# A decoder layer on one core: the order of the head's loads, and a fixed order of its work on the engines

## The chip, the cores and the metric

The kernel runs on one core of a Trainium2 chip. A core has five engines with queues of their own: TensorE (PE, with its weight loads as PEld), VectorE (DVE), ScalarE (ACT), GpSimd (POOL) and SyncE (SP), which here issues the DMAs. The metric is the device time of one execution in microseconds, median of several runs. The output has to agree with the float32 reference.

## The reference, cut to what matters

One decoder layer on 512 tokens of 1024 features, batch 1, all in float32:

```
mod = c @ w_ada + b_ada                      # 6 vectors of 1024: shift, scale, gate, twice
h   = rms_norm(x, g_pre_mix) * (1 + sc1) + sh1
proj = h @ w_in                              # [512, 1024] @ [1024, 2268]
o_nsa = nsa_attention(...)                   # 8 heads: compressed, selected and window branch, gated
o_dsa = dsa_attention(...)                   # 8 heads: an indexer picks the top 128 keys for each query
x = x + gt1 * rms_norm(concat(o_nsa, o_dsa) @ w_out, g_post_mix)
h = rms_norm(x, g_pre_ffn) * (1 + sc2) + sh2
y = relu(h @ w_up)**2 @ w_down               # 1024 -> 4096 -> 1024
out = x + gt2 * rms_norm(y, g_post_ffn)
```

The change concerns the way from the inputs to the first two column groups of `proj`: the parts of `mod` for shift and scale, `h`, and `h @ w_in` for the columns 1816 to 2268 ("A") and 512 to 1024 ("B").

## The kernel before, in words

**Arithmetic.** Every float32 matrix product of the projections is made of three passes on rounded operands. Each operand is split into a rounded part and a rest (`split`, L122 to L124: ACT casts the rounded part, DVE subtracts to get the rest), and the passes are rounded by rounded, rounded by rest, and rest by rounded. So each weight block of `w_in` costs a load, a cast on ACT (L123, names uhA, uhB, uh_D, uh_C) and a subtraction on DVE or POOL (L124, ulA, ulB, ul_D). The normalised input `h` is split too: `hh` (ACT, L305) and `hl` (DVE, L307 and L308).

**The head** is everything up to the end of the projections A and B, and it runs in steps k = 0 to 7, one for each slice of 128 of the 1024 features. For one k it does the following.

- `load_mod(k)` loads the columns of `w_ada` for shift and scale of this slice, four pieces of 256 KB (wm, L161). `load_a(k)` and `load_b(k)`, for even k, load the blocks of `w_in` for two slices (rwA 452 KB, L166; rwB 512 KB, L170).
- `mod_sums(k)` multiplies `c` with them on PE (mp, L286, 8 float32 matmuls that the profile shows as 16) and ACT copies the result out (macc, L291). `mod_mm(k)` sums over partitions with two small matmuls (mp, L297, shown as 4).
- `mod_h(k)`: DVE adds the bias and multiplies by the norm's weight (`as`, L301 and L302); with that as scale and bias ACT makes `hh` from the transposed slice xT, and DVE makes `hl`.
- `proj_pass` (L323): pA, 12 matmuls of 452 columns (3 passes by 4 row tiles), for step k; and pB, 9 matmuls of 512 columns (3 passes by 3 row tiles), for the step before. pB's fourth row tile comes behind the head, as pj_B.

Ahead of the loop x is loaded in four row tiles, squared and summed on ACT (L258), scaled on DVE (L262) and transposed on PE in 32 blocks (xTp, L268), with copies to xT on ACT (L269). Six of the eight slices are transposed as the row tiles come; slices 6 and 7 get a PSUM bank later.

**Behind the head** come pj_B, then the projections of the column chunks D (1024 to 1304), C (0 to 512) and E (1304 to 1816), each from `w_in_chunk` (loads L770), then the attention branches, the output projection and the MLP.

**What sets the order.** The program is written in Python calls, and a scheduler with a simulated timeline decides the order of the instructions on each engine from their dependences; in `before` it moves nearly all of them, the loads on SP too. `tc.issue_after(x)` makes what is emitted under it stand behind x; `tc.keep_in_program_order` keeps an instruction in the order of the program. Work of later stages is put into numbered slots of the program by the table PLAN and `place`. Buffers come from pools: `unit` (10 buffers of 512 KB), `raw` (4), k4 for x, and PSUM banks S (4), T (2) and O (2). A load waits until its buffer is free, and SP's queue stands at it meanwhile. Each DMA also waits for the DMA eight places ahead of it.

Of the kernel before, what the change touches and what calls it, by code (L numbers as in the profile page):

```python
# [69 lines left out]
def layer_kernel(  # L70
# [74 lines left out]
    for t in range(NT):  # L145
        xt = k4(f"x_{t}", F32)
        xs.append([xt[:, 0], xt[:, 1]])
        for i in range(2):
            SY.dma_start(xs[t][i], xv[t][:, i * 512:i * 512 + 512])
            if small:  # L150
                SY.dma_start(*small.pop(0))
# [113 lines left out]
    def x_transpose(k, tag):  # L265
        ps = bank(tag, f"xTp_{k}")
        for t in range(NT):
            last = PE.transpose(ps[:, t * P:(t + 1) * P], xs[t][k // 4][:, (k % 4) * P:(k % 4 + 1) * P], ident)  # L268
        A.copy(xT[k], ps)  # L269
        return last.ins  # L270
# [8 lines left out]
    def mod_sums(k):  # L279
# [11 lines left out]
        A.copy(acc, pv)  # L291
        macc[k] = (ps, acc)

    def mod_mm(k):
        ps, acc = macc[k]
        for v in range(2):
            PE.matmul(ps[:, 256 + v:257 + v], acc[:, v, :], ones32, start=True, stop=True)  # L297
        return ps[:, 256:258]

    def mod_h(k, ps):  # L300
# [4 lines left out]
        A.activation(hh[:, :, k, :], xT[k].rearrange("p (t q) -> p t q", q=P), AF.Identity,  # L305
                     scale=as1[:, 1, k:k + 1], bias=as1[:, 0, k:k + 1])
        V.tensor_scalar(h32, xT[k], as1[:, 1, k:k + 1], as1[:, 0, k:k + 1], op0=OP.mult, op1=OP.add)  # L307
        return lambda: V.tensor_tensor(hl[:, :, k, :], h3, hh[:, :, k, :].bitcast(F32), op=OP.subtract)  # L308
# [11 lines left out]
    def proj_pass(ps, t, k, w, n, i):  # L320
        hi, lo = w[k // 2]
        l, r = ((hh, hi), (hh, lo), (hl, hi))[i]
        PE.matmul(ps[:, :n], l[:, t, k, :], r[:, k % 2, :n],  # L323
                  start=(k == 0 and i == 0), stop=(k == KT - 1 and i == 2))
# [8 lines left out]
    mod_sums(0)  # L333
    last = [x_transpose(k, "S") for k in range(4)][-1]
    with tc.issue_after(last):
        mp = mod_mm(0)
    split_a(0)
    rt_ops = rope_tables()
    psA = [bank("S", f"pA_{t}") for t in range(NT)]
    psB = []  # L340
    for k in range(KT):
        mod_h(k, mp)()
        if k + 1 < KT:
            mod_sums(k + 1)
        if k + 3 < KT:
            if k % 2 == 1:
                load_a(k + 1)
            load_mod(k + 3)
            if k % 2 == 1:
                load_b(k + 1)  # L350
        if k % 2 == 1 and k + 1 < KT:
            if k + 3 >= KT:
                load_a(k + 1)
                load_b(k + 1)
            split_a(k + 1)
        if k % 2 == 0:
            split_b(k)
# [224 lines left out]

    def cmp_load(nm):
# [180 lines left out]
    def w_in_chunk(c0, c1, nm, eng=V):  # L764
# [16 lines left out]
    for f in lD:  # L781
        f()
# [12 lines left out]
    for t in range(NT + 2):  # L795
# [8 lines left out]
        sD=sD, cl=[lambda: cmp_load("k"), lambda: cmp_load("v")], lC=lC, sC=sC, lE=lE, sE=sE,  # L804
# [5 lines left out]
        tk1=tk[1], tk2=tk[2], tk3=tk[3], g1=g1s, a2=a2s, sh2=sh2s)  # L810
# [389 lines left out]
```

## Time and profile before

| | us |
|---|---|
| median of 3 runs | 730.72 (730.03 to 732.52) |
| the profiled execution | 730.62, of which the span from the first to the last instruction is 728.9 |
| head: first pA matmul, first of pj_B | 23.53, 76.99 |
| busy: PE, DVE, ACT, POOL | 686.2, 458.0, 331.8, 128.9 |

A row of the timeline reads: start, length, engine, line, operation, output<-inputs, shapes, count, and in brackets how long the engine was idle before it and for what. "PE mp L286 <- DVE as L301: 2.5, 3, 1.5" in the waits means that PE stood 2.5 us in 3 waits ahead of such matmuls, 1.5 at the longest, until an `as` of DVE was there. In the windows view, the clock is the rate granted to PE as a share of its full one; waits and chain name the program's tiles with their numbers left out.

### The profile page before, as it was taken

The numbers are of one execution on the slowest core, as the hardware profiler recorded it, in microseconds if no ns is written. First come the engines' busy times: TensorE is split into PE (matmuls) and PEld (weight loads), VectorE is DVE, ScalarE is ACT, GpSimd is POOL, SyncE is SP. The second block draws the span as 40 slices with busy tenths as digits, with TensorE's granted clock in tenths as the row PEclk, the third lists the DMA queues.
The fourth block names the chain that finished last, engine by engine and source line by source line (L and its number), as shares of the span: only waits on it lengthen the run. The fifth ranks groups of instructions, "written<-read, shape, count | busy, mean of one in ns | idle before, by whom it ended". The sixth has DMA issues, their size and how long they took to land.

```text
span 728.9 us, 9985 instructions
## 1 busy us (share of the span) xinstructions
PE 686.2 (94%) x3601; PEld 535.1 (73%) x3601; DVE 458.0 (63%) x978; ACT 331.8 (46%) x691; POOL 128.9 (18%) x196
## 2 busy tenths in 40 slices
PE   4898989979998999799999999999999999999995
PEld 2676978857664666465699888888888888788884
DVE  4345548989998989775675463653734455443547
ACT  5343685534896569644564323232331332323222
POOL 3000195635524125122020000000000000000003
PEclk9999999999998999999999999999999999999998
DMA  8997430422316761462123351533424133331202
GB/s 246 300 304 246 115 88 2 114 69 78 117 27 176 176 144 29 121 227 87 58 88 103 101 169 63 174 115 116 147 60 169 58 116 115 89 114 59 86 1 115
DMA packets 67611, 87.15 MB, mean 120 GB/s; under 512 B 3973, under 2 KB 38889, under 8 KB 67562
## 3 DMA queue, kind: packets, MB, share of 16 engines
q1 hardware_dynamic: 67562, 86.52, 39.6%
q8 instruction: 28, 0.46, 0.3%
q14 instruction: 21, 0.17, 0.1%
HBM read 84.40 MB, written 2.10 MB: 119 GB/s over the span
## 4 chain that ended last, share of the span: by engine, by line
PE 74%; DVE 12%; DMA 4%; POOL 3%; issue 2%; ACT 2%; SPq 2%; POOLq 0%; DVEq 0%; ACTq 0%
PE up L1113 23%; PE dn L1154 22%; PE op L1006 6%; PE O L905 3%; PE pj_E L323 3%; PE pA L323 2%; DMA wm<-in_w_ada_dram 2%; PE pj_C L323 2%; DVE wk L570 1%; PE pB L323 1%; DVE m L567 1%; SPq L161 1%; PE tp_d L899 1%; DVE P_d L894 1%; DMA rwA<-in_w_in_dram 1%
## 5 line engine op out<-in xcount | busy, mean ns | idle before, releaser
L1113 PE MATMUL up<-hh,uh_U 128*128 128x512 f32 (+1 forms) x288 | 104.6, 366 | 0.6 <-ACT hh L123 0.6
L1113 PE MATMUL up<-hh,ul_U 128*128 128x512 f32 (+1 forms) x288 | 104.9, 366 | 0.0
L1113 PE MATMUL up<-hl,uh_U 128*128 128x512 f32 (+1 forms) x288 | 104.0, 366 | 0.0
L1154 PE MATMUL dn<-uh_D,al 128*128 128x512 f32 x256 | 99.6, 389 | 0.0
L1154 PE MATMUL dn<-uh_D,ah 128*128 128x512 f32 x256 | 98.7, 391 | 0.0
L1154 PE MATMUL dn<-ul_D,ah 128*128 128x512 f32 x256 | 98.5, 389 | 0.0
L124 DVE TENSOR_TENSOR ul_D<-rw_D,uh_D 128x1024 fp32r<-128x1024 f32 (+1 forms) x35 | 41.2, 1180 | 47.5 <-ACT uh_D L123 45.4
L1160 DVE TENSOR_TENSOR y<-dn,y 128x512 f32<-128x512 f32 x56 | 38.1, 688 | 48.6 <-PE dn L1154 48.6
L206 POOL TENSOR_SCALAR ms<-sy 128x1 f32<-128x1 f32 x4 | 3.6, 909 | 341.6 <-ACT fj L1133 341.6
L1113 PEld LDWEIGHTS up<-hh,uh_U 128*128 128x128 f32 x288 | 54.3, 188 | 9.7 <-ACT hh L123 0.9
L1117 ACT ACTIVATE rl<-up 128x512 f32<-128x512 f32 x32 | 19.1, 596 | 92.7 <-PE dn L1154 59.2
L1113 PEld LDWEIGHTS up<-hh,ul_U 128*128 128x128 f32 x288 | 54.3, 189 | 8.8
L1113 PEld LDWEIGHTS up<-hl,uh_U 128*128 128x128 f32 x288 | 53.7, 189 | 8.9 <-DVE hl L124 0.2
L123 ACT CAST uh_U<-rw_U 128x1024 fp32r<-128x1024 f32 x32 | 33.6, 1051 | 55.2 <-PE dn L1154 51.9
L123 ACT CAST uh_D<-rw_D 128x1024 fp32r<-128x1024 f32 (+1 forms) x36 | 36.3, 1010 | 46.2 <-PE up L1113 37.5
L1154 PEld LDWEIGHTS dn<-uh_D,al 128*128 128x128 f32 x256 | 48.1, 188 | 10.2 <-issue 0.2
L1154 PEld LDWEIGHTS dn<-uh_D,ah 128*128 128x128 f32 x256 | 48.1, 188 | 10.2 <-issue 0.2
L1154 PEld LDWEIGHTS dn<-ul_D,ah 128*128 128x128 f32 x256 | 48.0, 188 | 10.0
L124 DVE TENSOR_TENSOR ul_U<-rw_U,uh_U 128x1024 fp32r<-128x1024 f32 x32 | 39.1, 1221 | 10.9 <-ACT uh_U L123 10.0
L1118 DVE TENSOR_TENSOR rl<-rl 128x512 f32<-128x512 f32 x32 | 22.0, 689 | 34.9 <-ACT rl L1117 34.9
L123 ACT CAST ah<-rl 128x512 fp32r<-128x512 f32 x32 | 19.9, 621 | 29.3 <-DVE rl L1118 29.2
L124 DVE TENSOR_TENSOR al<-rl,ah 128x512 fp32r<-128x512 f32 x32 | 22.0, 688 | 11.0 <-ACT ah L123 11.0
(407 smaller groups left out, 1473.4 us busy)
## 6 DMA issues: line engine op xcount, KB each, us to landing
rw_U<-in_w_up_dram SPq DMA_DIRECT2D x32, 512.0 KB, 4.5
rw_D<-in_w_down_dram SPq DMA_DIRECT2D x32, 512.0 KB, 3.7
wm<-in_w_ada_dram SPq DMA_DIRECT2D x32, 256.0 KB, 6.3
wv_g<-in_w_ada_dram SPq DMA_DIRECT2D x8, 512.0 KB, 4.6
rwo_a<-in_w_out_dram SPq DMA_DIRECT2D x16, 256.0 KB, 4.9
wv_a<-in_w_ada_dram SPq DMA_DIRECT2D x8, 512.0 KB, 3.7
rwo_b<-in_w_out_dram SPq DMA_DIRECT2D x16, 256.0 KB, 4.9
wv_sh<-in_w_ada_dram SPq DMA_DIRECT2D x8, 512.0 KB, 4.2
```

The source lines that it names most:

```text
L123: A.copy(hi, src)
L124: eng.tensor_tensor(lo, src, hi.bitcast(F32), op=OP.subtract)
L161: mod_in[k].append(SY.dma_start(wt[hf][:, v], wa[:, hf * 4:hf * 4 + 4, v * D + k * P:v * D + (k + 1) * P]))
L323: PE.matmul(ps[:, :n], l[:, t, k, :], r[:, k % 2, :n], start=(k == 0 and i == 0), stop=(k == KT - 1 and i == 2))
L567: mx = V.max(m8, work[t])
L905: mm = [PE.matmul(O[j][g * 64:(g + 1) * 64, :], vn[kb][:, self.vsl[g]:self.vsl[g] + 64], pts[kb, g][0], start=(first and kb == 0), stop=(l ...
L1006: PE.matmul(stt["ps"], l[:, kk, :], r[:, kk % 2, :], start=(kk == 0 and i == 0), stop=(kk == 7 and i == 2))
L1113: PE.matmul(pv[:, t0:t1, :], l[:, k % 2, fs], r[:, t0:t1, k, :], start=(n == 0), stop=(n == 23))
L1117: A.activation(rl, ps, AF.Relu)
L1118: V.tensor_tensor(rl, rl, rl, op=OP.mult)
L1154: PE.matmul(ps, l[:, t * P:(t + 1) * P], r[:, f % 2, :], start=(n == 0), stop=(n == 11))
L1160: V.tensor_tensor(ya, ps, ya, op=OP.add)
```

## The change

Four things are changed, all in or around the head.

1. The loads. x comes in four loads of a whole row tile (512 KB) instead of eight halves, and the six small loads go from SP's queue to ACT's. The loads of wm, rwA and rwB stay in the order of the program, which is now wm0, rwA0, wm1, rwB0, wm2, rwA2, wm3, rwB2 and so on to rwB6. The loads of chunk D stand behind rwB6; those of the compression weights (`cl`) and of the output gate (`g1`: g and wv_g) behind D's last, C's behind these.
2. The transposes. The copies of xT alternate between ACT (even k) and DVE (odd k). In the program the transposes of slices 1 to 3 stand behind `mod_h(0)`.
3. The order in the loop. `behind(done, f)` emits f under `issue_after` of each instruction of `done`. `mod_mm(k+1)` is put behind the last pA matmul of step k, the nine pB behind that, and the sums of the step after next ahead of the following row of pA; for k = 0 and 1 the sums stand behind the second pass. The splits of the next A and B blocks stand behind `mod_h`, and those of chunk D behind the last `mod_h`.
4. `x_transpose`, `mod_sums`, `mod_mm`, `mod_h`, `load_b`, `proj_pass` and the chunk's `load` return the instructions that this needs. The arithmetic is the same.

```diff
-        for i in range(2):
-            SY.dma_start(xs[t][i], xv[t][:, i * 512:i * 512 + 512])
-            if small:
-                SY.dma_start(*small.pop(0))
+        SY.dma_start(xt.rearrange("p a n -> p (a n)"), xv[t])
+    for dst, src in small:
+        A.dma_start(dst, src)
...
-                mod_in[k].append(SY.dma_start(wt[hf][:, v], wa[:, hf * 4:hf * 4 + 4, v * D + k * P:v * D + (k + 1) * P]))
+                src = wa[:, hf * 4:hf * 4 + 4, v * D + k * P:v * D + (k + 1) * P]
+                mod_in[k].append(tc.keep_in_program_order(SY.dma_start(wt[hf][:, v], src)))
...
-        A.copy(xT[k], ps)
-        return last.ins
+        return A.copy(xT[k], ps) if k % 2 == 0 else V.tensor_copy(xT[k], ps)
...
+    def behind(done, f, *args):
+
+        with ExitStack() as es:
+            for ins in done:
+                es.enter_context(tc.issue_after(ins.ins))
+            return f(*args)
+
+    first = mod_sums(0)
+    first_T = x_transpose(0, "S")
+    mp, _ = mod_mm(0)
+    behind((first, first_T), split_a, 0)
...
     for k in range(KT):
-        mod_h(k, mp)()
-        if k + 1 < KT:
-            mod_sums(k + 1)
+        done = mod_h(k, mp)
+        if k == 0:
+            for q in (1, 2, 3):
+                behind(done, x_transpose, q, "S")
+            psA = [bank("S", f"pA_{t}") for t in range(NT)]
+        if k % 2 == 0 and k + 2 < KT:
+            load_a(k + 2)
+        elif k % 2 == 1 and k + 1 < KT:
+            head_end = (load_b(k + 1),)
         if k + 3 < KT:
             load_mod(k + 3)
...
+        if 1 < k < KT - 1:
+            mod_sums(k + 1)
         for ps in (0, 1, 2):
             for t in range(NT):
-                proj_pass(psA[t], t, k, wA, 452, ps)
+                mm = proj_pass(psA[t], t, k, wA, 452, ps)
+            if k < 2 and ps == 1:
+                done += (behind((mm,), mod_sums, k + 1),)
+        if k % 2 == 0:
+            behind(done, split_b, k)
+        elif k + 1 < KT:
+            behind(done, split_a, k + 1)
...
         if k + 1 < KT:
-            mp = mod_mm(k + 1)
+            mp, mm = behind((mm,), mod_mm, k + 1)
         for t in range(3):
             if k > 0:
-                proj_mm(psB[t], t, k - 1, wB, 512)
+                behind((mm,), proj_mm, psB[t], t, k - 1, wB, 512)
...
+    d_loads = [behind(head_end, f) for f in lD]
+    sD = [lambda f=f: behind(done, f) for f in sD]
...
-        sD=sD, cl=[lambda: cmp_load("k"), lambda: cmp_load("v")], lC=lC, sC=sC, lE=lE, sE=sE,
+        sD=sD, cl=[held(lambda: cmp_load("k")), held(lambda: cmp_load("v"))], lC=lC, sC=sC, lE=lE, sE=sE,
```

Here `held(f)` is `behind` with the last load of D. How the rows stand on the engines now is shown at three places; numbers behind a name are buffer numbers.

On PE, at the start, where the transposes (xTp) of the last two x tiles meet the first sums (mp from wm). Before:

```order
L268 MATMUL xTp_276<-ident,x_82 128x128
L268 MATMUL xTp_282<-ident,x_82 128x128
L268 MATMUL xTp_202<-ident,x_87 128x128
...
L268 MATMUL xTp_282<-ident,x_87 128x128
L286 MATMUL mp_191<-wm_90,c_sb 32x256 x4
L286 MATMUL mp_191<-wm_91,c_sb 32x256 x4
L297 MATMUL mp_191<-ones_113,macc_200 128x1 x2
```

and with the change (x_76 and x_78 are the last two tiles):

```order
L268 MATMUL xTp_280<-ident,x_74 128x128
L285 MATMUL mp_187<-wm_86,c_sb 32x256 x4
L285 MATMUL mp_187<-wm_87,c_sb 32x256 x4
L268 MATMUL xTp_198<-ident,x_76 128x128
...
L268 MATMUL xTp_274<-ident,x_78 128x128
L268 MATMUL xTp_280<-ident,x_78 128x128
L296 MATMUL mp_187<-ones_109,macc_196 128x1 x2
```

The first sums stood behind the transposes of all four tiles and now stand ahead of those of the last two.

On PE in the loop, at the end of step 3 and the start of step 4, where the sums' last matmul (L297, now L296) meets pA, pB and the next sums. Before:

```order
L323 MATMUL pA_236<-uhA_323,hl_177 128x452
L323 MATMUL pB_349<-uhB_386,hl_177 128x512
L323 MATMUL pB_350<-uhB_386,hl_177 128x512
L323 MATMUL pB_351<-uhB_386,hl_177 128x512
L297 MATMUL mp_423<-ones_113,macc_432 128x1 x2
L286 MATMUL mp_500<-wm_380,c_sb 32x256 x4
L286 MATMUL mp_500<-wm_381,c_sb 32x256 x4
L323 MATMUL pA_233<-uhA_444,hh_176 128x452
```

and with the change:

```order
L323 MATMUL pA_238<-uhA_335,hl_173 128x452
L296 MATMUL mp_452<-ones_109,macc_461 128x1 x2
L323 MATMUL pB_345<-uhB_400,hh_172 128x512
...
L323 MATMUL pB_347<-uhB_400,hl_173 128x512
L285 MATMUL mp_510<-wm_367,c_sb 32x256 x4
L285 MATMUL mp_510<-wm_368,c_sb 32x256 x4
L323 MATMUL pA_235<-uhA_475,hh_172 128x452
```

Between the sums' last matmul and the next pA stood the next sums alone; now the nine pB and the sums stand there.

On SP, the loads of the second half of the head. Before:

```order
L161 DMA wm_380<-in_w_ada_dram 128x4x128 x2
...
L736 DMA g_1617<-in_g_post_mix_dram 128x1024
L711 DMA wv_g_1623<-in_w_ada_dram 128x4x256
L161 DMA wm_436<-in_w_ada_dram 128x4x128 x2
L711 DMA wv_g_1628<-in_w_ada_dram 128x4x256
L161 DMA wm_381<-in_w_ada_dram 128x4x128 x2
L166 DMA rwA_434<-in_w_in_dram 128x2x452
...
L770 DMA rw_D_696<-in_w_in_dram 128x2x280
L161 DMA wm_512<-in_w_ada_dram 128x4x128 x2
L166 DMA rwA_567<-in_w_in_dram 128x2x452
L170 DMA rwB_569<-in_w_in_dram 128x2x512
```

and with the change:

```order
L166 DMA rwA_496<-in_w_in_dram 128x2x452
L161 DMA wm_498<-in_w_ada_dram 128x4x128 x2
L161 DMA wm_499<-in_w_ada_dram 128x4x128 x2
L170 DMA rwB_554<-in_w_in_dram 128x2x512
L782 DMA rw_D_692<-in_w_in_dram 128x2x280
...
L748 DMA g_1613<-in_g_post_mix_dram 128x1024
L723 DMA wv_g_1619<-in_w_ada_dram 128x4x256
L723 DMA wv_g_1624<-in_w_ada_dram 128x4x256
L782 DMA rw_C_764<-in_w_in_dram 128x2x512
```

The loads g and wv_g and the first of D stood among the head's loads; now the last of the head's, rwB6, stands ahead of D, and D ahead of g, wv_g and C.

More of the change, by code (lines that the diff above doesn't have):

```diff
@@ L165, in load_a @@
         raw_a[k] = unit(f"rwA{k}", F32)
-        SY.dma_start(raw_a[k][:, :, :452], wiv[:, k:k + 2, 1816:2268])
+        tc.keep_in_program_order(SY.dma_start(raw_a[k][:, :, :452], wiv[:, k:k + 2, 1816:2268]))
     def load_b(k):
         raw_b[k] = unit(f"rwB{k}", F32)
-        SY.dma_start(raw_b[k], wiv[:, k:k + 2, 512:1024])
+        return tc.keep_in_program_order(SY.dma_start(raw_b[k], wiv[:, k:k + 2, 512:1024]))
     load_mod(0)
@@ L267, in x_transpose @@
         for t in range(NT):
-            last = PE.transpose(ps[:, t * P:(t + 1) * P], xs[t][k // 4][:, (k % 4) * P:(k % 4 + 1) * P], ident)
-        A.copy(xT[k], ps)
-        return last.ins
+            PE.transpose(ps[:, t * P:(t + 1) * P], xs[t][k // 4][:, (k % 4) * P:(k % 4 + 1) * P], ident)
+        return A.copy(xT[k], ps) if k % 2 == 0 else V.tensor_copy(xT[k], ps)
     hh = ht("hh", "hh_1")
@@ L290, in mod_sums @@
         acc = m2(f"macc_{k}")[:, 0:256].rearrange("p (v n) -> p v n", v=2)
-        A.copy(acc, pv)
         macc[k] = (ps, acc)
+        return A.copy(acc, pv)
     def mod_mm(k):
@@ L296, in mod_mm @@
         for v in range(2):
-            PE.matmul(ps[:, 256 + v:257 + v], acc[:, v, :], ones32, start=True, stop=True)
-        return ps[:, 256:258]
+            mm = PE.matmul(ps[:, 256 + v:257 + v], acc[:, v, :], ones32, start=True, stop=True)
+        return ps[:, 256:258], mm
     def mod_h(k, ps):
@@ L322, in proj_pass @@
         l, r = ((hh, hi), (hh, lo), (hl, hi))[i]
-        PE.matmul(ps[:, :n], l[:, t, k, :], r[:, k % 2, :n],
-                  start=(k == 0 and i == 0), stop=(k == KT - 1 and i == 2))
+        return PE.matmul(ps[:, :n], l[:, t, k, :], r[:, k % 2, :n],
+                         start=(k == 0 and i == 0), stop=(k == KT - 1 and i == 2))
     def proj_mm(ps, t, k, w, n):
@@ L332, in layer_kernel @@
     columns()
[L333 to L337, printed above, removed]
+    def behind(done, f, *args):
[7 more added lines that the diff above has]
+    behind((first, first_T), split_a, 0)
     rt_ops = rope_tables()
-    psA = [bank("S", f"pA_{t}") for t in range(NT)]
     psB = []
     for k in range(KT):
-        mod_h(k, mp)()
-        if k + 1 < KT:
-            mod_sums(k + 1)
+        done = mod_h(k, mp)
[7 more added lines that the diff above has]
+            head_end = (load_b(k + 1),)
         if k + 3 < KT:
-            if k % 2 == 1:
-                load_a(k + 1)
             load_mod(k + 3)
[L349 to L357, printed above, removed]
         for _ in range(4):
@@ L581, in layer_kernel, with held @@
     csrc = {"k": (cmp_pe_k, cmp_w1_k, cmp_w2_k), "v": (cmp_pe_v, cmp_w1_v, cmp_w2_v)}
+    def held(f):
+        return lambda: behind(d_loads[-1:], f)
     def cmp_load(nm):
@@ L809, in layer_kernel @@
         ck3=[lambda: cmp_gelu("k"), lambda: cmp_out("k")], cv3=[lambda: cmp_gelu("v"), lambda: cmp_out("v")],
-        tk1=tk[1], tk2=tk[2], tk3=tk[3], g1=g1s, a2=a2s, sh2=sh2s)
+        tk1=tk[1], tk2=tk[2], tk3=tk[3], g1=[held(f) for f in g1s[:3]] + g1s[3:], a2=a2s, sh2=sh2s)
     slots = {n: [] for n in range(40)}
```

9 lines of the change are left out of this document (4 added, 5 removed).

## The prediction, made before the changed kernel ran

> **What bounds the kernel now.** I read the page's totals first, then the windows view, the waits of the stretch in question, its chain of waits and its timeline.
>
> ```profile
> span 728.9 us, 9985 instructions
> PE 686.2 (94%) x3601; PEld 535.1 (73%) x3601; DVE 458.0 (63%) x978; ACT 331.8 (46%) x691; POOL 128.9 (18%) x196
> ```
>
> TensorE is busy 94% of the span. A gain of some size must come from PE's idle time or from time at a lower clock. The windows view says where those lie. The columns are the window, its length, the busy time (with the instruction count) of PE, weight loads, DVE, ACT and POOL, the granted clock, the DMA share and the GB/s.
>
> ```profile
> 29.55:64.00 34.45, 31.72 (x211) 24.41 (x209) 16.36 (x31) 15.05 (x23) 1.76 (x1) 1.00 0.99 291
> 64.00:68.00 4.00, 4.00 (x19) 3.25 (x12) 1.34 (x2) 1.01 (x3) 0.00 (x0) 0.59 0.97 342
> 68.00:77.00 9.00, 7.63 (x38) 6.55 (x37) 2.01 (x5) 3.00 (x6) 0.00 (x0) 0.99 0.20 76
> 140.00:320.00 180.00, 165.70 (x981) 110.79 (x980) 160.13 (x491) 116.25 (x308) 66.99 (x82) 0.95 0.42 116
> ```
>
> ```profile
> 29.14 0.66 PE L268 MATMUL xTp<-ident,x 128*128 128x128 f32 x4
> 29.55 1.06 PE L323 MATMUL pA<-uhA,hh 128*128 128x452 f32 x4
> 76.99 0.39 PE L323 MATMUL pj_B<-uhB,hh 128*128 128x512 f32 x1
> ```
>
> These rows of the timeline (start, length) give the borders: step k=1 of pA begins at 29.55, and the head is over at 76.99, 47.44 us later, when pj_B begins. From 29.55 on PE is idle for 2.73 us before 64 and for 1.37 us after 68, in sum 4.10. In 64 to 68 it runs at 0.59, which costs 0.41 of 4.00 = 1.64 us. So 5.74 us of the head after 29.55 are neither work nor full clock. The two waits named for PE there add up to the idle time:
>
> ```profile
> PE mp L286 <- DVE as L301: 2.5, 3, 1.5
> PE pA L323 <- ACT hh L305: 1.6, 2, 1.4
> ```
>
> The chain of waits shows how they come about (start, length, what):
>
> ```profile
> 42.13 6.25 DMA rwA<-in_w_in_dram
> 48.46 0.94 ACT uhA L123
> 49.41 0.73 ACT hh L305
> 50.18 1.92 PE pA L323 x8
> ...
> 52.44 0.94 PE pA L323 x4
> 53.37 2.21 PE pB L323 x9
> 55.58 1.00 PE mp L286 x16
> ...
> 58.43 1.39 PE pB L323 x6
> ...
> 61.35 0.35 PE mp L297 x4
> 61.70 1.38 DVE ul_D L124 x2
> 63.08 0.08 DVE as L301
> ...
> 71.46 0.82 ACT hh L305
> ...
> 77.16 0.92 PE pj_B L323 x4
> ```
>
> Three stalls. At 48 us ACT stands at the cast of rwA4, whose load landed late, and hh of that step queues behind it. At 61.70 the vector `as` queues on DVE behind two splits of chunk D that nobody needs yet, and the next sums wait for it. At 71.46 the last hh stands in the chain itself: between the last mm and the pA of step 7 no pB is left to cover it.
>
> **The change, part by part.** *The loop from pA(1) on.* The directly ordered loop puts mod_mm(k+1) behind the twelve pA of step k, then nine pB and the next sums. After the mm the next step needs `as` and hh, about 0.36 + 0.81 and the hand-overs, 1.5 us in all. Nine pB (2.21) and one sums (1.00) are 3.2 us of cover; before, the mm often stood last and had one sums, 1.0, as cover. So the waits on `as` and hh should go, which removes 4.10 us, and with the idle of 1.52 us ahead of it the slow window (1.64) probably goes too: it is the only slow one in the head. If it does not, the gain is 1.64 smaller; that end is in the range. DVE keeps its splits, but behind `hl`, and D's behind the last `hl`: they move to where the next `as` is 3 us away.
>
> Does the data come in time? A step takes 2.7 (pA: 1.92 + 0.94, the shorter repeats less) + 2.2 + 1.0 + 0.35 = 6.2 us. It needs four pieces of wm, 1.05 MB, and half of one rwA and one rwB (loads with their KB and the us to landing; then the GB/s in slices of 2.25 us from 0 to 90):
>
> ```profile
> wm<-in_w_ada_dram SPq DMA_DIRECT2D x32, 256.0 KB, 6.3
> rwA<-in_w_in_dram SPq DMA_DIRECT2D x4, 452.0 KB, 7.2
> wv_g<-in_w_ada_dram SPq DMA_DIRECT2D x2, 512.0 KB, 5.6
> GB/s 29 242 277 217 252 314 330 303 325 313 290 291 291 327 339 261 235 215 313 332 329 321 332 321 346 367 294 137 201 349 373 20 0 0 0 256 320 291 65 0
> ```
>
> With rwB's 512 KB that is 1.05 + 0.24 + 0.26 = 1.55 MB in 6.2 us, 250 GB/s; the row of 29.55 to 64 moved 291. Before, the two wv_g (1.05 MB, 3.6 us at 291), g and D's first chunk ran ahead of rwA6 and rwB6; now they stand behind. So I price the supply at nothing, with the transfers behind the work as cover; the bound, if it moved only the 217 GB/s of a slow slice at the start, is 1.55/0.217 = 7.1 us a step, 0.9 us times six steps = 5.4 us lost.
>
> From pA(1) to the head's end the after program also has work that before stood ahead of pA(1): six pB of k=0 (1.39), sums(2) (1.00) and the transposes of slice 7 (0.6). So this part takes 47.44 - 4.10 - 1.64 + 1.39 + 1.00 + 0.60 = 44.7 us.
>
> *The start, up to pA(1).* Here the rows are (start, length):
>
> ```profile
> 1.24 0.42 SPq L151 DMA_DIRECT2D c_sb<-in_c_dram  x1
> 14.82 1.54 PE L268 MATMUL xTp<-ident,x 128*128 128x128 f32 x6 [2.02 <-DVE x L262]
> 16.29 1.94 PE L286 MATMUL mp<-wm,c_sb 128*32 128x256 f32 x16
> 18.77 1.01 PE L297 MATMUL mp<-ones,macc 128*128 128x1 f32 x4 [0.55 <-ACT macc L291]
> 19.89 0.16 DVE L301 TENSOR_TENSOR as<-mp,colb 128x2 f32<-128x2 f32 x1 [2.44 <-PE mp L297]
> 20.17 1.10 DVE L124 TENSOR_TENSOR ulA<-rwA,uhA 128x904 fp32r<-128x904 f32 x1
> 20.34 0.81 ACT L305 ACTIVATE hh<-xT,as 128x512 fp32r<-128x512 f32 x1 [0.78 <-DVE as L302]
> 21.18 0.54 DVE L307 TENSOR_SCALAR h<-xT,as 128x512 f32<-128x512 f32 x1
> 21.83 0.69 DVE L308 TENSOR_TENSOR hl<-h,hh 128x512 fp32r<-128x512 f32 x1
> 28.14 1.07 PE L286 MATMUL mp<-wm,c_sb 128*32 128x256 f32 x16
> ```
>
> The new order has sums(0) ahead of the transposes of x tiles 2 and 3 (12 rows, 2 x 1.54). Sums(0) starts when wm0 has landed: x and wm0 are 3.15 MB, at some 0.28 MB/us (the slices from the second on) from about 2 us that is 13.4; the bound on the other side is 16.3, where it stood. From it: 1.94 + 3.08 + 1.01 and `as` give hh0 at 19.9 to 22.8, against 20.34. To pA(1): hl0 is 2.25 us behind the start of hh0 (0.54 + 1.10 + 0.69), then pass 3 of two tiles and the five pA behind it (1.6), sums(1) 1.07, one pA 0.22, a transpose group 0.6, the mm 0.35, and the open chain to hh1 of 1.5, since at k=0 no pB stands there yet: 7.55 us. So pA(1) comes at 27.45 with PE at full rate and wm0 early. [...] I take the middle, 28.6, with 27.45 and 32.7 (late and slow) as bounds.
>
> [...]
>
> *The loads at the top.* x in four loads instead of eight and the small ones on ACT's queue: ten issues fewer on SP, 0.42 us each, 4.2 in all. What it is worth is within wm0's 13.4 to 16.3: the 9.5 us for x's bytes cover the issues of wm0 in the early case. On ACT the six issues, 2.5 us, stand ahead of the squares of x; that can make tile 0 up to 2.5 us later, but tile 3 waits for its bytes, so 0. *xT copies*: four of 0.6 us go from ACT to DVE, three of them ahead of as(1); they run under pA(0) and sums(1), so 0, and at most 0.6 if the last is still running when mm(1) ends.
>
> *What is behind the head.* PE's order is the same from pj_B on for 217 rows, through pj_D and pj_C, and again through the whole MLP; only in between are rows shuffled. So an earlier head end should carry through.
>
> ```profile
> 74.28 1.05 ACT L123 CAST uh_C<-rw_C 128x1024 fp32r<-128x1024 f32 x1 [2.01 <-PE pA L323]
> 89.03 0.32 POOL L401 TENSOR_TENSOR ra_Bc<-pjB,rsin 128x64 f32<-128x64 f32 x1 [28.33 <-PE skp_kA L417]
> ```
>
> POOL's rope waits for PE's skp_kA at 89 and so follows the head. The danger is C: its loads now stand behind g, wv_g and w_k and need D's buffers, and the cast of C0 on ACT has copies of pA banks behind it, which pj_D needs. I estimate C0 between the new head end and 2.4 us behind it; the banks are needed 5 us behind it, so 0, with 1 us as bound.
>
> **The sum.** pA(1) 28.6 + 44.7 = 73.3, against 76.99: 3.7 us earlier. The profiled execution took 730.62 (span 728.9 and 1.7 around it); the median of the runs, 730.72, is the same. Forecast 730.6 - 3.7 = **726.9**.
>
> **The rivals.** *PE at full rate at once*: 27.45 + 44.7 = 72.15, 4.8 gained, 725.8. [...] Against: the row of 16.29 with transposes just ahead of it. *The start eats the gain*: wm0 lands only at 16.3 and sums(0) has 12 transposes behind it instead of in front. pA(1) then stands at 30.3 (warm) to 32.7 (slow), the head ends 75.0 to 77.4: 728.6 to 731.0, in the middle 729.8. For it: before had all tiles done at 16.36 and sums running at once. Against: the slices above show no stop of the DMA before 16, and wm0 had ten issues more ahead of it.
>
> *The loads do not keep up* (the order is there, its data not): the 217 GB/s case, 5.4 - 3.7 = 1.7 lost, about 732.3; against it, most slices of the loop stand at 290 or above, though one shows 215. *Slower through the middle*: from 140 to 320 DVE is busy 160.1 of 180 and PE idle 14.3; the rows of DVE, ACT and PE are shuffled a little there. If DVE's new order opens two more gaps like that at 61.70, each with 1.52 idle and a 0.59 window of 1.64, 6.3 us go: 730.6 - 3.7 + 6.3 = 733.2. It decides from 3.7 us on. For it: that stretch's clock of 0.95 says such windows come easily (0.05 x 180 = 9 us). Against: the moves are of a few rows each, and could close a gap as well.
>
> **Chances.** Forecast 0.47 (726.9), warm at once 0.15 (725.8), start 0.18 (729.8), loads 0.06 (732.3), middle 0.14 (733.2). 0.3%, 2.2 us, is about what a measurement of this kernel tells from no change: 728.5 and 732.9 are the borders. Faster 0.61 (the first two, less a little), same 0.25, slower 0.14. The range: 722.8 (warm, and 3 us closed in the middle) to 732.0 (late and slow start, 1 us for C); the forecast's own is 725.8 (27.45) to 728.2 (29.9).
>
> **What would show it.** Right: pj_B's first matmul at 72 to 75; no wait of mp on `as` and at most one, 1.5 us at k=0, of pA on hh; the granted clock at 1.00 from 29 to the head's end; rwB6's landing by some 52 us; the rows from 77 on the same distance earlier through 320. The start is right if hh0 stands at 19.9 to 20.5 and pA(1) near 28.6. Wrong: pA(1) past 31, a wait on a wm load, ACT standing at uh_C for over 5 us, or a PE idle time from 140 to 320 well above 14.3, with the head's gain then gone again by 320.

## The result, and the profile after

The changed kernel takes 726.04 us (median of 14 runs, 724.12 to 730.4) against 730.56 us of the kernel before on the same chip (14 runs, 728.59 to 732.79). The ratio is 0.9942, with a 95% interval of 0.9921 to 0.9962. The forecast was 726.9 in a range of 722.8 to 732.0, faster. The profiled execution took 724.70. Three slow executions, two of the kernel before (739.96 and 1127.28 us) and one of the kernel with the sums of step 1 early (1121.82), are in no median or mean below.

The totals of its page:

```profile
span 723.0 us, 9982 instructions
PE 684.1 (95%) x3601; PEld 532.8 (74%) x3601; DVE 460.8 (64%) x982; ACT 328.6 (45%) x687; POOL 131.8 (18%) x196
```

The windows view (window, length, busy time of PE, weight loads, DVE, ACT, POOL, granted clock, DMA share, GB/s) shows the loop as it was meant: PE busy for all of 44 us, at full clock.

```profile
20.00:29.00 9.00, 7.54 (x63) 5.28 (x64) 4.24 (x8) 3.72 (x6) 0.00 (x0) 1.00 1.13 317
29.00:73.00 44.00, 44.00 (x267) 34.77 (x266) 23.86 (x49) 17.96 (x32) 1.40 (x1) 1.00 0.87 252
```

In the waits view from 23 to 75 us, PE has one wait left, that of the open chain to step 1, and ACT stands for 5.8 us ahead of the cast of C:

```profile
ACT uh_C L123 <- DMA rw_C<-in_w_in_dram: 5.8, 1, 5.8
...
PE pA L323 <- ACT hh L304: 1.5, 1, 1.5
```

The chain of waits in the same stretch is PE alone, in the order that the change wrote down (sums' last matmul L296 behind pA, nine pB, the next sums L285):

```profile
56.37 1.00 PE mp L285 x16
57.37 2.67 PE pA L323 x12
60.04 0.34 PE mp L296 x4
60.37 2.17 PE pB L323 x9
62.55 2.47 PE pA L323 x12
65.02 4.13 PE pB L323 x18
69.15 5.45 PE pj_B L323 x24
```

The first pj_B matmul stands at 68.98, 8.0 us earlier than before. The span is only 5.9 us shorter. The first instances of the same tiles on PE say where the rest went: pj_D is 8.0 us earlier (74.42 against 82.46), the first of pj_E 8.3 (126.81 against 135.14), the first tp_d of the attention's last part, those that read hh_d, 5.7 (276.07 against 281.73), and from there on the lead stays at 5.7 to 5.9. So the lead is carried whole to the middle, and 2.85 us of it are lost between sc, the first scores of the compressed branch (172.17 before, 163.66 after), and tp_d. The windows of this stretch, before:

```profile
172.17:193.75 21.58, 20.63 (x134) 15.78 (x133) 19.76 (x76) 14.30 (x47) 12.86 (x22) 0.92 0.19 63
193.75:241.78 48.03, 44.44 (x269) 27.22 (x266) 45.43 (x156) 37.50 (x107) 15.78 (x17) 0.93 0.48 121
241.78:281.73 39.95, 39.33 (x228) 27.02 (x228) 33.40 (x92) 27.71 (x69) 11.25 (x12) 1.00 0.47 120
```

and after, between the same tiles:

```profile
163.66:187.61 23.95, 22.23 (x137) 17.08 (x136) 21.47 (x80) 14.76 (x48) 13.20 (x22) 0.86 0.14 45
187.61:236.75 49.14, 45.03 (x265) 27.79 (x265) 43.86 (x154) 36.69 (x102) 15.80 (x17) 0.90 0.42 125
236.75:276.07 39.32, 39.08 (x228) 26.82 (x227) 34.14 (x92) 28.04 (x71) 12.35 (x12) 1.00 0.46 113
```

I call length x (1 - granted clock) the clock loss. It is 1.73 + 3.36 = 5.1 us in this stretch before and 3.35 + 4.91 = 8.3 us after. The difference, 3.2 us, is more than the 2.85 us; PE's idle time is 5.2 and 6.1.

At the start the sums of step 0 and what follows them stand like this (timeline: start, length):

```profile
12.75 1.92 PE L285 MATMUL mp<-wm,c_sb 128*32 128x256 f32 x16
14.60 1.53 PE L268 MATMUL xTp<-ident,x 128*128 128x128 f32 x12
15.96 0.50 PE L296 MATMUL mp<-ones,macc 128*128 128x1 f32 x4
17.03 0.81 ACT L304 ACTIVATE hh<-xT,as 128x512 fp32r<-128x512 f32 x1
24.82 1.09 PE L323 MATMUL pA<-uhA,hh 128*128 128x452 f32 x4 [1.46 <-ACT hh L304]
```

The sums still ran at about half rate (1.92 us, where the next ones, at 21.11, take 1.07), the twelve transposes behind them at full rate: 1.53 us, where the forecast had 3.08.

### The profile page after: what moved, and what is told of

The parts are those of the page before. It is cut to its first block, busy times and chain, and to the rows that moved or that the text cites. A ratio compares the mean times of both kernels' runs of the same rounds, so it can differ in the third digit from the quotient of the medians.

```text
span 723.0 us, 9982 instructions
## 1 busy us (share of the span) xinstructions
PE 684.1 (95%) x3601; PEld 532.8 (74%) x3601; DVE 460.8 (64%) x982; ACT 328.6 (45%) x687; POOL 131.8 (18%) x196
## 4 chain that ended last, share of the span: by engine, by line
PE 76%; DVE 11%; DMA 4%; ACT 4%; POOL 3%; issue 2%; POOLq 0%; ACTq 0%; SPq 0%; DVEq 0%
PE up L1125 23%; PE dn L1166 22%; PE op L1018 5%; PE pA L323 3%; PE pj_E L323 3%; PE O L917 3%; PE pB L323 2%; DVE wk L578 1%; DVE m L575 1%; DMA rwo_b<-in_w_out_dram 1%; PE mp L285 1%; PE tp_d L911 1%; PE pj_C L323 1%; PE tp_s L911 1%; DMA wv_g<-in_w_ada_dram 1%
## 5 line engine op out<-in xcount | busy, mean ns | idle before, releaser
L1129 ACT ACTIVATE rl<-up 128x512 f32<-128x512 f32 x32 | 19.1, 598 | 92.6 <-PE dn L1166 59.2
L1166 PEld LDWEIGHTS dn<-uh_D,al 128*128 128x128 f32 x256 | 48.1, 188 | 10.2 <-issue 0.2
```

The costliest lines, as they stand in the source:

```text
L1129: A.activation(rl, ps, AF.Relu)
L1166: PE.matmul(ps, l[:, t * P:(t + 1) * P], r[:, f % 2, :], start=(n == 0), stop=(n == 11))
```

## The experiments

All are edits of the changed kernel. The table has the ratio to the kernel before on the same chip; where pA of step 1 and pj_B begin in the one profile; and, as means over all timed runs, the clock loss and the time without it (time - span x (1 - granted clock)). That last figure must be read with care: up to the moment at which a trace first records full rate (14.5 us in the first profile of the change, 23.8 before, 5.7 in the kernel with PE warmed) the clock's record says 1.00 although the durations show about half rate (sums of 1.92 and 1.94 us that take 1.07 later in the first two, transposes of 0.42 us that take 0.27 later in the third), so that part of a slow start counts as time without clock loss.

| kernel | median us | ratio [95%] | pA(1) | pj_B | clock loss | time without it |
|---|---|---|---|---|---|---|
| before (three sets of runs on two chips, 17 to 29 each) | 731.2 to 733.0 | 1 | 29.55 | 76.99 | 16.2 to 17.6 | 714.9 to 715.8 |
| the change, first runs | 726.04 | 0.9942 [0.9921, 0.9962] | 24.82 | 68.98 | 18.1 | 708.5 |
| the change again | 726.91 | 0.9938 [0.9919, 0.9957] | 27.93 | 73.61 | 18.4 | 708.6 |
| x in halves | 730.41 | 0.9968 [0.9942, 0.9994] | 28.72 | 72.88 | 17.0 | 713.3 |
| small loads on SP | 729.23 | 0.9959 [0.9938, 0.9979] | 27.41 | 71.58 | 17.8 | 711.4 |
| first sums last | 725.44 | 0.9929 [0.9904, 0.9954] | 26.46 | 70.64 | 16.4 | 710.1 |
| xT copies on ACT | 726.89 | 0.9931 [0.9907, 0.9956] | 27.33 | 73.02 | 19.0 | 708.7 |
| sums' last matmul behind pB | 729.54 | 0.9961 [0.9931, 0.9990] | 25.89 | 74.74 | 18.7 | 711.5 |
| engine order free | 728.54 | 0.9947 [0.9920, 0.9974] | - | 76.42 | 16.8 | 711.9 |
| loads' order free | 730.16 | 0.9964 [0.9933, 0.9996] | 27.65 | 73.33 | 19.7 | 710.6 |
| no holding back | 729.41 | 0.9965 [0.9948, 0.9982] | 26.93 | 72.64 | 19.1 | 710.2 |
| PE warmed | 727.56 | 0.9943 [0.9928, 0.9958] | 26.16 | 71.83 | 20.2 | 707.2 |
| sums of step 1 early | 724.99 | 0.9896 [0.9873, 0.9919] | 24.12 | 68.29 | 14.6 | 709.6 |
| the same again | 723.12 | 0.9881 [0.9861, 0.9900] | 25.01 | 69.18 | 14.6 | 708.8 |

### The changed kernel once more

No edit.

> The changed kernel once more, unaltered, on the chip of the runs beside it. If its gain lies in the head and in work and idle time, not in luck with the clock (theory A), the time without what the lower clock costs (span x (1 - granted clock)) is about 708.5 again, some 6 us below the same figure of the kernel before, pA of step 1 begins between 24.8 and 27.7, and the loop takes 44.2 us and 1.7 more for each slow-clock stretch in it. If the 69.0 of the first profile was luck (rival), pj_B stands past 72.

The loop takes 73.61 - 27.93 = 45.68 us, 1.5 more than in the first profile, and PE is never idle in it; the start is 3.1 us later. Timeline and windows of this execution show why (the same program, the same order):

```profile
13.10 1.93 PE L285 MATMUL mp<-wm,c_sb 128*32 128x256 f32 x16 [0.76 <-DMA wm<-in_w_ada_dram]
14.96 2.82 PE L268 MATMUL xTp<-ident,x 128*128 128x128 f32 x12
...
18.79 0.81 ACT L304 ACTIVATE hh<-xT,as 128x512 fp32r<-128x512 f32 x1 [0.60 <-DVE as L301]
```

```profile
20.00:24.00 4.00, 4.00 (x15) 2.48 (x18) 2.74 (x5) 0.56 (x2) 0.00 (x0) 0.66 1.11 314
24.00:28.00 4.00, 2.54 (x26) 1.56 (x18) 1.39 (x4) 2.52 (x4) 0.00 (x0) 0.91 1.12 318
28.00:32.00 4.00, 4.00 (x24) 2.71 (x24) 1.23 (x3) 0.00 (x0) 0.00 (x0) 0.57 1.15 305
```

The twelve transposes take 2.82 instead of 1.53, and PE runs at about half rate in two more stretches up to 32. Both readings have a part: the time without clock loss is 708.6 as expected, and pj_B past 72 says that the 69.0 of the first profile was a lucky start. These two profiles of the head differ by 4.6 us, so a single one can't be trusted to less than that.

### x in halves again

```diff
-        SY.dma_start(xt.rearrange("p a n -> p (a n)"), xv[t])
-    for dst, src in small:
-        A.dma_start(dst, src)
+        for i in range(2):
+            SY.dma_start(xs[t][i], xv[t][:, i * 512:i * 512 + 512])
+            if small:
+                SY.dma_start(*small.pop(0))
```

> The changed kernel, but x comes in eight halves with the six small loads between them on SP again; by that the sums of step 0 fall behind the transposes of all four x tiles again. With the change, pA of step 1 begins at 24.82 us and pj_B at 68.98. If the start gained by the form of x's loads and the sums' place ahead of the last two tiles (theory A: 26.55 minus 24.82 = 1.7 us of the 8.0), pA of step 1 comes 1.5 to 3 us later, the loop still takes 44.2, and pj_B stands at 70.5 to 72. If the start's gain comes from the engine order alone (rival), pA of step 1 stays at 24.8 to 25.3 and pj_B at 69 to 69.5. Total against the kernel before: 2 to 5 us less by A.

```profile
16.19 1.93 PE L286 MATMUL mp<-wm,c_sb 128*32 128x256 f32 x16
...
18.67 1.01 PE L297 MATMUL mp<-ones,macc 128*128 128x1 f32 x4 [0.55 <-ACT macc L292]
...
20.24 0.81 ACT L305 ACTIVATE hh<-xT,as 128x512 fp32r<-128x512 f32 x1 [0.78 <-DVE as L302]
```

In the timeline, hh of step 0 stands at 20.24, where before had 20.34; with the change it was 17.03, and 18.79 in the slow start. The loop takes 44.16 again. So this part brings 1.5 us against the slow start and 3.2 against the lucky one, and up to hh of step 0 the start is that of before again: as far as that row tells, the form of the loads, with the place of the sums that follows from it, is the start's whole gain. pA(1) is 0.8 us later than in the slow start, and pj_B at 72.88 is a little past theory A's 72. By the ratios the timed runs lose 2 us of the change's gain. In this profile even the 4.1 us by which pj_B is earlier than before are gone at the end (span 728.8 against 728.9), although the order of PE behind the head is that of before; the section on the middle comes back to this.

### The small loads on SP

```diff
-        A.dma_start(dst, src)
+        SY.dma_start(dst, src)
```

> The changed kernel with x in whole tiles, but the six small loads on SP behind x and ahead of wm. They cost 6 x 0.42 = 2.5 us of SP. If the byte rate sets when wm of step 0 lands (theory A), the sums of step 0 start within 0.5 us of 13.0 and the time without clock loss is 708.6 to 709.5; then what the halves of x cost in the earlier run comes from the halves. If SP's issues set it (rival), the sums start at 14.5 to 16 and the time without clock loss is 710.5 or more.

The sums of step 0 start at 14.18, between the two expectations: the six issues cost 1.1 to 1.4 us there, half of their 2.5. The scheduler also moved ten of the last twelve transposes ahead of the sums, and `as` comes at 17.77, between the 16.58 and the 18.33 of the two profiles of the change. By the ratios the timed runs lose 1.2 to 1.5 us of the change's gain. The time without clock loss, 711.4, lies where the rival had it (710.5 or more). So SP's issues do matter at the start, but how the loss divides between them and the slow rate isn't shown.

### The first sums last

```diff
...
-    first = mod_sums(0)
     first_T = x_transpose(0, "S")
+    first = behind((last_T[0],), mod_sums, 0)
```

> The changed kernel with the sums of step 0 put behind the transposes of slice 0, so behind those of x tiles 0 to 2 and some of tile 3; loads as with the change. If the sums' place ahead of the last two tiles made the start earlier (theory A), the vector as of step 0 comes 0.7 us later (17.3 against 16.6) and pj_B 0.5 to 1 us later. If the place decides whether PE runs at full rate by then (rival), as comes 2 us later or more and pj_B at 71 or past it.

`as` comes at 17.24, 0.66 us later than the lucky start, as theory A said, and PE was at full rate by then (sums 1.12). pA(1) waits 2.43 us for hh and comes 1.6 later; pj_B at 70.64 lies between the two expectations. One profile alone doesn't settle it, since in the six profiles with the change's order at the start `as` comes anywhere from 16.36 to 18.33. But the time without clock loss, 710.1 against 708.6, says the same: the sums' place is worth some 1.5 us. The median is no worse than that of the change, for the clock loss is 2 us smaller; the section on the middle comes back to this too.

### The xT copies on ACT

```diff
-        return A.copy(xT[k], ps) if k % 2 == 0 else V.tensor_copy(xT[k], ps)
+        return A.copy(xT[k], ps)
```

> The changed kernel with all eight xT copies on ACT again. If they cost nothing where they are (theory A, as forecast), as and hh of steps 0 and 1 stand where they stand with the change, within 0.3 us at equal clock, and the time without clock loss is 708.6 within 0.6. If ACT was the engine on the path at the start (rival), four copies of 0.6 us stand ahead of hh of step 0 or 1 and pA of step 1 comes 1 to 2 us later at equal clock.

The time without clock loss is 708.7, the loop 45.69 with the same slow stretch as the second profile of the change. The copies' engine is worth nothing, as forecast.

### The sums' last matmul behind pB

```diff
...
-        if k + 1 < KT:
-            mp, mm = behind((mm,), mod_mm, k + 1)
         for t in range(3):
             if k > 0:
                 behind((mm,), proj_mm, psB[t], t, k - 1, wB, 512)
+                lastb = lastmm[0]
+        if k + 1 < KT:
+            mp, mm = behind((lastb if k > 0 else mm,), mod_mm, k + 1)
```

> The changed kernel, but the sums' last matmul of a step stands behind the nine pB again instead of directly behind the twelve pA; loads and start as with the change. If the gain of the loop comes from pB covering the way from that matmul over the vector as to hh (theory A), 1.5 us has only the next sums (1.0) as cover in steps 1 to 6 and nothing before step 7: about 0.5 x 5 + 1.5 = 4 us more, pj_B at 73, and a slow-clock window of 1.7 us may come back. If the loads' order made the loop's gain (rival), pj_B stays at 69.

From its waits of PE in the head:

```profile
PE pA L323 <- ACT hh L304: 2.8, 2, 1.5
PE mp L285 <- DVE as L300: 1.5, 5, 0.3
```

Five waits of 0.3 us and one more of 1.3 ahead of step 7 are back, 2.8 us in all, and the loop takes 48.85 against 45.68 in the change at a similar clock (0.97 and 0.96). Theory A's 4 us was a little high, since the sums hide all but 0.3 of the 1.5 in a step, not all but 0.5. In the timed runs it is 2.9 us of the time without clock loss, and 1.4 to 1.7 by the ratios. The rival had pj_B at 69; it stands at 74.74. This is the mechanism of the loop, shown alone: on PE, this kernel differs from the change only in the place of these matmuls and of one instruction behind the head.

### The engine order free

```diff
-    first = mod_sums(0)
-    first_T = x_transpose(0, "S")
+    mod_sums(0)
+    tr = [x_transpose(k, "S") for k in range(4)][-1]
...
-            mp, mm = behind((mm,), mod_mm, k + 1)
+            mp, mm = mod_mm(k + 1)
...
-                behind((mm,), proj_mm, psB[t], t, k - 1, wB, 512)
+                proj_mm(psB[t], t, k - 1, wB, 512)
...
-    sD = [lambda f=f: behind(done, f) for f in sD]
```

> The changed kernel with its loads (x in whole tiles, fixed order, D, g and wv_g held) and the xT copies on both engines, but with nothing fixed in the loop: the scheduler places the sums, their last matmul, pB and the splits as it likes, and the sums' last matmul stands behind or between the pB again. If the fixed engine order is worth most of the loop's 6.3 us (theory A), the waits of PE on as and hh come back with 2 to 4 us and pj_B stands at 71 to 74. If the loads are worth it all (rival), pj_B stays within 0.5 of 69.

```profile
PE mp L285 <- DVE as L300: 4.1, 2, 3.8
PE pA L323 <- ACT hh L304: 2.3, 2, 1.4
```

The waits are back, 6.4 us from 20 us on (4.1 before, from 23.5 on), more than theory A had, and pj_B stands at 76.42, where it stood before the change. So the loads in order without the engines in order bring next to nothing to the head. The total is nevertheless 0.5% below that of before. In its one profile most of the gain lies behind the head: from pj_B to the end it takes 650.2 us, against 651.9 before. It has an order of its own in the middle, which no other kernel here has; whether that is the reason isn't shown.

### The loads' order free, and nothing held back

```diff
-                mod_in[k].append(tc.keep_in_program_order(SY.dma_start(wt[hf][:, v], src)))
+                mod_in[k].append(SY.dma_start(wt[hf][:, v], src))
...
-    d_loads = [behind(head_end, f) for f in lD]
+    d_loads = [f() for f in lD]
...
-        return lambda: behind(d_loads[-1:], f)
+        return f
```

(and the same for rwA and rwB; the second kernel has the last two edits only)

> The changed kernel without the fixed order of the loads and without holding D, g and wv_g back: on SP g, wv_g, and the compression weights stand among wm, rwA and rwB again, as before. The order on PE is as with the change. If the loop needs both (theory A), 1.05 MB of wv_g and 0.5 MB of g ahead of rwA and wm cost about 1.6 MB at 0.31 MB/us = 5 us of supply, of which 1.5 to 4 show, as a wait on rwA's cast or on wm between 35 and 65; pj_B at 70.5 to 73. If the engine order alone made the gain (rival), pj_B stays at 69.

> The changed kernel with wm, rwA and rwB in their fixed order, but D not held behind rwB6 and g, wv_g and the compression weights not held behind D: 1.5 MB of g and wv_g stand ahead of rwA2 now, which is 4.9 us at 0.31 MB/us. The earlier run with all of the loads' order free cost 2.1 us of the time without clock loss. If holding back the later stages' loads is what matters (theory A), this run costs as much or more, 710.5 to 713, with waits on rwA2 or wm around 30 to 40. If the fixed order among the head's own loads is what matters (rival), this run is at 708.6 to 709.2.

The loop takes 45.68 and 45.71 us, exactly that of the change in its second profile, and PE has the one wait of 1.5 and no other:

```profile
PE pA L323 <- ACT hh L304: 1.5, 1, 1.5
```

(The row reads the same for both.) So with the engines in a fixed order the loads' order costs nothing that a profile of the head shows, though 1.5 MB of g and wv_g stand ahead of rwA2 in the second kernel and 1.0 MB in the first: no wait on rwA or wm came, and theory A fails in the head. Yet the timed runs are 1.6 to 2.1 us slower without clock loss, with standard errors of 0.4. Where that lies isn't shown; executions in which a load came late, or slow starts, would both do it. It stays open.

### PE warmed ahead of the first transpose

```diff
...
+    for _ in range(24):
+        PE.transpose(cps[:, P:2 * P], ident, ident)
     PE.transpose(cps[:, :P], rows, ident)
```

> The changed kernel with 24 more transposes of the identity on PE, into unused columns of a PSUM bank, ahead of the first transpose; they are extra work that nothing reads, and run from about 2 to 8 us, when PE has nothing else. [...]

```profile
13.28 1.07 PE L287 MATMUL mp<-wm,c_sb 128*32 128x256 f32 x16 [0.93 <-DMA wm<-in_w_ada_dram]
```

```profile
14.00:18.00 4.00, 2.31 (x25) 1.79 (x17) 2.35 (x9) 2.67 (x5) 0.00 (x0) 1.00 1.09 300
18.00:22.00 4.00, 3.90 (x11) 2.65 (x11) 3.74 (x9) 0.81 (x2) 0.00 (x0) 0.67 1.13 315
...
26.00:30.00 4.00, 3.84 (x20) 2.84 (x24) 1.45 (x3) 0.11 (x1) 0.00 (x0) 0.57 1.12 322
```

The sums run in 1.07 and `as` comes at 15.61, 1 us earlier than in the first profile of the change. But the timeline of the start (PE) and the windows speak against the extra work as the reason:

```profile
2.18 4.54 PE L218 MATMUL cps<-ident 128*128 128x128 f32 x24 [2.18 <-POOL ident masks.py:199]
8.77 0.30 PE L219 MATMUL cps<-ident,rows 128*128 128x128 f32 x1 [2.06 <-DMA rows<-in_g_pre_ffn_dram]
9.15 3.19 PE L270 MATMUL xTp<-ident,x 128*128 128x128 f32 x12
...
9.12:12.53 3.41, 3.09 (x12) 2.29 (x12) 3.10 (x12) 2.08 (x8) 3.04 (x6) 0.50 0.95 262
```

The extra transposes take 0.42 us each at first and 0.27 at the end, and the clock's record begins with full rate at 5.7, 3.5 us after the first of them. Then PE idles for 2.06 us, the granted clock from 9.12 to 12.53 is 0.50, and the first twelve transposes of x take 3.19, as without the extra work. The sums behind them run in 1.07 also in two kernels that have no extra work ahead of them, the one with the sums' last matmul behind pB (at 13.17) and the second profile of the next kernel (at 12.77).

Nor does the earlier `as` reach the next step. ACT comes to hh of step 0 at 17.04, as in the first profile of the change (17.03), because the cast of the first A block stands ahead of it in both:

```profile
16.19 0.95 ACT L123 CAST uhA<-rwA 128x904 fp32r<-128x904 f32 x1
17.04 0.81 ACT L306 ACTIVATE hh<-xT,as 128x512 fp32r<-128x512 f32 x1
```

PE fell back once more at 19.4, behind a stretch in which it was busy for 2.31 of 4 us and never idle for more than 1.69 at a time, and again at 26. pA(1) stands at 26.16 and pj_B at 71.83, between the 68.98 and the 73.61 of the two profiles of the change. The clock loss of the runs is the largest of all, 20.2, but in this kernel it counts a slow stretch at 9 us that comes ahead of the record's start in the others. So warming this early brings nothing that these profiles show.

### The sums of step 1 early

```diff
...
+        if k == 0:
+            done += (mod_sums(1),)
...
+            if k == 0 and ps == 0:
+                mp1, mm1 = behind((mm,), mod_mm, 1)
...
-        if k + 1 < KT:
+        if k == 0:
+            mp, mm = mp1, mm1
+        elif k + 1 < KT:
             mp, mm = behind((mm,), mod_mm, k + 1)
```

> The changed kernel with the sums of step 1 ahead of pA of step 0 and their last matmul behind the first pass of that pA, so that the last open wait, PE 1.46 us for hh of step 1 ahead of pA of step 1, has two passes of pA over it. If wm of step 1 has landed by the time (theory A), pA of step 1 begins 1.0 to 1.5 us earlier against the unaltered kernel at equal clock (23.4 to 23.8) and pj_B at 67.5 to 68. If wm of step 1 lands later than 17.9 (rival), the sums stall ahead of pA(0) and pj_B gains nothing or comes later.

> The kernel with the sums of step 1 ahead of pA of step 0, once more. In the first run its ratio to the kernel before was 0.9896, that of the unaltered changed kernel on the same chip 0.9938, but its time without clock loss was 709.6 against 708.6, so the lead came from a smaller clock loss (14.6 against 18.4 us). If the lead is the kernel's (theory A), it has a ratio below 0.992 again and a clock loss of 14 to 16. If it was the clock's chance (rival), the clock loss is 16 to 19 and the ratio 0.993 to 0.996, no better than the changed kernel.

The waits of PE in the second profile, from 17 us to the head's end:

```profile
PE mp L285 <- DMA wm<-in_w_ada_dram: 2.3, 1, 2.3
PE pA L323 <- ACT hh L304: 0.8, 1, 0.8
```

The wait for hh shrinks from 1.46 to 0.8 us, but a wait for wm of step 1 stands ahead of it now (1.2 and 2.3 us in the two profiles): most of that time PE waited for hh of step 0 before, so part of the gain stays. pj_B comes at 68.29 and 69.18. It is the fastest kernel of the study, 0.9881 [0.9861, 0.9900] and 0.9896 [0.9873, 0.9919], and on the chip of the second of these the change with its copies on ACT had 0.9931. So the lead is the kernel's, as theory A of the second run had it. But it isn't the lead that the edit was made for: pA(1) and pj_B come later than the 23.4 to 23.8 and 67.5 to 68 of the first run's theory A, for wm of step 1 comes about when its rival had it (the sums start at 17.79 and 17.89 us, the rival's border was 17.9), and the time without clock loss is no shorter than that of the change (709.6 and 708.8 against 708.6). The clock loss is smaller, 14.6 us both times.

### The middle, over all the kernels

Why is that loss smaller, when only the head was touched? The scheduler gives the middle, from pj_E to the last attention transposes, on PE one of two orders in all but one of these kernels. Six have the order of before to the row (before, x in halves, small loads on SP, first sums last, PE warmed, sums of step 1 early). Five have that of the change (the change, copies on ACT, sums' last matmul behind pB, loads' order free, nothing held back; between pj_E and tp_d 273 of 822 matmuls stand at another place, two more for one of them). The engine order left free gave a third. Nobody chose these orders: the edits are all in the head.

The stretch from the first sc to the first tp_d of the last part, which has the same matmuls in both, takes 109.0 to 110.8 us in the seven profiles of the first group and 111.9 to 113.1 in the six of the second, 109.8 and 112.4 in the mean. Its clock loss is 3.3 to 5.1 us in the one and 8.3 to 8.7 in the other. For the first sums last, for example:

```profile
166.12:187.91 21.79, 20.84 (x135) 15.82 (x134) 19.84 (x76) 14.41 (x48) 12.87 (x22) 0.92 0.19 62
187.91:235.88 47.97, 44.38 (x269) 27.01 (x266) 45.41 (x156) 37.51 (x107) 15.79 (x17) 0.93 0.49 119
```

These rows are those of before almost digit for digit, while the head is that of the change but for the sums' place. So the length of this stretch goes with its order.

It doesn't follow that the order costs 2.6 us of the total. The two orders part right behind the start of pj_E, 46 of the matmuls that stand elsewhere lie ahead of sc, and four profiles of the first group (x in halves, small loads on SP, sums of step 1 early) take 1.5 to 2.0 us longer than before from pj_E to sc. Over the whole of it, from pj_E to tp_d, the groups take 146.6 to 149.8 and 147.3 to 149.9 us, 147.9 and 149.0 in the mean, and from pj_B to the end 653.9 in the mean both. What the order does go with is the clock loss: from pj_E to tp_d it is 6.8 us in six of the seven profiles and 10.2 in five of the six (8.5 in the other two). That is most of what the kernel with the sums of step 1 early has less than the change (14.6 against 18.4), and the likely reason why the first sums last, with a head 1.6 us longer, is no slower. In other kernels of the first group idle time of PE takes its place (x in halves: 13 us from pj_E to tp_d, against 10.3 before). No run changes the order of the middle alone, so what it is worth stays open.

## Why the prediction came out right, step by step

The forecast, 726.9, was right in time and sign, and the second profile of the change is nearly its picture: pj_B at 73.61 (73.3 forecast), median 726.91. The loop, which carries the gain, was right in mechanism and size. That the total came so close is luck in part: the start came out better than forecast and the middle worse, and the two cancelled.

- **The loop** was right. 44.7 us were forecast from pA(1) on; 44.16 were measured, and 45.68 with a slow stretch that costs 1.7. The 4.10 us of idle time went to nothing. The run with the engine order free shows that the fixed order does it, and the one with the sums' last matmul behind pB that it does it by the cover that was named.
- **The slow window** at 64 was to go with the idle time (1.64 us). That failed as a saving. It is not in the first profile, but another of 1.7 us stands in the second, and over all runs the clock loss grew from 16.2 to 17.6 us up to 18.1 to 18.4. With the gap gone, slow stretches turned up elsewhere.
- **The start** was mis-sized: pA(1) was put at 28.6, 2 us later than the equal work before, and hh of step 0 at 19.9 or later, where 17.03 and 18.79 were measured. In the six profiles whose start has the change's order on PE (the two of the change, copies on ACT, sums' last matmul behind pB, loads' order free, nothing held back), it stands at 24.82 to 27.93, 26.8 in the mean, and 26.55 would have been no loss. The sums took 1.07 to 1.94 where 1.94 was put, the transposes behind them 1.53 to 2.82 instead of 3.08, the mm 0.50 to 0.65 instead of 1.01, and the sums could start at 12.8 to 13.2 instead of 13.4. The bounds (27.45 and 32.7) were too late at the lower end: four of the six profiles lie below it. (The terms of the 7.55 add up to 7.59; that changes nothing.) The 2.4 us by which 29.9 lies above 27.45 (and 32.7 above 30.3) were my estimate of a slow rate, and no run shows them; in their place the runs showed the two profiles of the change 3.1 us apart at pA(1) (24.82 and 27.93), with the granted clock at 1.00 from 14.5 us to pj_B in one, and at 0.66 from 20 to 24 and 0.57 from 28 to 32 in the other.
- **Loads at the top** priced at "within wm0's 13.4 to 16.3" was right as a bound; the halves and the small loads on SP put the sums at 16.19 and 14.18. **Supply at nothing** was right for the head, also with 1.5 MB more ahead of it. **Copies at nothing**: right.
- **Carried through 1:1** held to pj_E (8.0 to 8.3 us), and failed in the middle, where 2.85 and 2.39 us went in the two profiles of the change. The rival of the middle named the place and slow stretches after moved rows, but at 6.3 us and behind new gaps of PE; PE's idle time from 140 to 320, the sign that was named, was 11.9 and 13.9 us, no more than the 14.3 of before, so the slow stretches came without new gaps of that kind. ACT did stand at uh_C for 5.8 us, which was named as a sign of failure; it cost nothing, for PE was busy for 20.00 of the 20 us from 69 to 89, and the price of 0 was right.

The sum as it was, between the same tiles, in us earlier (+) or later (-) than before. For the start, 26.55 is what pA(1) would be with the work that the change moved behind it (29.55 less 3.0):

| | start | loop | pj_B to pj_E | to sc | sc to tp_d | behind | span |
|---|---|---|---|---|---|---|---|
| forecast | -2.05 | +5.74 | 0 | 0 | 0 | 0 | +3.7 |
| first profile | +1.73 | +6.27 | +0.32 | +0.18 | -2.85 | +0.24 | +5.9 |
| second profile | -1.38 | +4.75 | +1.60 | +0.19 | -2.39 | +0.32 | +3.1 |

The +1.60 of the second profile is one slow stretch less between pj_B and pj_E (56.55 us against 58.15). The medians of the timed runs, 4.5 and 4.3 us below those of the kernel before, lie between the two.

## What to carry to other kernels

Put the last short operation of a dependent chain directly behind the work that frees it, and the long independent work behind that: here nine matmuls cover 1.5 us that one sums could not, and the kernel with the loads alone in order gained 0.6 us in its head. When an edit shortens the start of a program whose order a scheduler makes, compare the order and the granted clock of everything behind it too; in the two profiles of the change 2.85 and 2.39 us of the head's lead were gone again 100 us later. Take more than one profile before a stage is timed to a few us, and compare stages between the same tiles, with idle time and clock loss apart, and with borders outside of what was reordered: here a stretch that began inside it showed 2.6 us where the whole had 1.1.

## What the runs showed of the hardware

Two profiles of one program differ by 4.6 us at the end of a 70 us stage, with the same order and the same waits, because PE's rate changes at other moments: full rate from 14.5 us in one, 0.66 from 20 to 24 and 0.57 from 28 to 32 in the other. In the warmed kernel a lower clock came back (0.67 in the window from 18 to 22) behind a stretch with no idle time longer than 1.7 us (busy 2.31 of 4), and the full rate recorded at 5.7 was gone again by 9 (0.50 from 9.12 to 12.53), behind 2.06 us of idle time. Loss to the lower clock was 14.6 to 20.2 us of a run of 725, more than three times what this change gained, and from pj_E to tp_d it was 6.8 us in most profiles of one order and 10.2 in most of another order of the same instructions. In the first 20 us the clock's record says 1.00 while sums take 1.93 instead of 1.07, so there the durations are the better witness.
